# Weights' sums of the last three down passes made in DRAM by adding DMAs, ahead of time

## The chip, the cores and the metric

One Trainium2 chip, one of its cores. The metric is the device time of one execution in microseconds (us); the median of several runs counts.

## The reference, cut to what matters

One layer of a diffusion backbone over 1024 tokens of 1024 channels: a token mixer (Fourier groups and gated DeltaNet heads), then a ConvGLU channel mixer. The change lies in the channel mixer:

```python
p = h @ w_up_l                      # 1024 x 1024 by 1024 x 5632
val, gate = p[..., :D_FF], p[..., D_FF:]          # D_FF = 2816
gate = lax.conv_general_dilated(gate.reshape(bsz, rows, GRID_W, D_FF), w_dwc_l[:, :, None, :], ...)
return (jax.nn.silu(gate) * val) @ w_down_l       # 2816 x 1024
```

All arrays are float32, and so is the result.

## The kernel before, in words

Every matrix product is made of three: both operands are split into a high part (rounded to the type float32r) and the low rest, and `mm3` (L189) issues high x high (L191), high x low (L192) and low x high (L193). The high part is a cast on ACT, the low part a subtraction (`sub_l`, L164, its line in the profile is L165), on DVE or on POOL (GpSimd).

**Up products** (`ffn`, L1426, the loop at L1695). The hidden channels are 22 tiles of 128 (NF). For a channel tile f, seven products p = 1 to 7 over quarters of the operands replace eight (a Strassen-like scheme): `load(f)` (L1623) reads two pieces of w_up of 512 KB each on SP's queue, into the two buffers `raw` (even f) or into pages (odd f); `prepw(f, p)` (L1635) makes the sum of weights that p needs, on DVE or POOL, casts it on ACT into a buffer `wh` (four buffers) and subtracts on POOL into `wl`. It runs three products ahead (WA). A product is 12 matmuls. The tile x[5] of a channel tile gets x[7] added on POOL after p == 7 (L1729). DVE also makes the 3x3 convolution (L1472) and the gating, and 17 of the 22 gated tiles `g` are stored to DRAM (`gd`, L1482).

**Down products** (L1562 to L1617 and the loop at L1787). The product of the gated tiles with w_down is cut in the same way into 7 passes of 11 channels (NJ). A pass uses sums of two parts of the gate and sums of two blocks of w_down; `PASSES` lists them, as (half, part, sign) each:

```python
(((0, 0, 1), (1, 1, 1)), ((0, 0, 1), (1, 1, 1))), \
(((0, 1, 1), (1, 1, -1)), ((1, 0, 1), (1, 1, 1))), \
(((1, 0, 1), (0, 0, -1)), ((0, 0, 1), (0, 1, 1)))
```

These are the last three (numbers 4, 5 and 6 in the code): all three need a sum of two blocks of w_down. `prep(n)` (L1586) prepares channel j of a pass: it loads the blocks of w_down, 128 x 512, 256 KB each, on SP's queue (L1599), adds them on DVE (L1601), casts (L1608) and subtracts on DVE (L1609); then the same for the gate's parts: a sum on DVE (L1613), a cast (L1616), a subtraction on DVE (L1617). It is written five channels ahead of the products `mm(n, t)` (L1778), which make 12 matmuls per channel into four banks, t = 0 to 3. After a pass the banks are added up on DVE; the last sums of each output tile, its norm and the residual are in `early` (L1750) and `out` (L1756), which sit in a list `late` and are issued between channels. For the last six channels of the last pass the products are written bank by bank: all six for t = 0, then an addition of that bank (L1810) and `out(1, t)`, then t = 1 and so on.

Loads, gate parts, splits and results share a ring of 36 pages of 512 KB (`pg`, L143); `wh` and `wl` have four buffers each.

The order of the instructions on each engine is not fixed by the text alone. When the program is built, an ordering pass places instructions by when their operands and buffers are expected to be ready, and among those by the order of the text. `tc.issue_after(x)` holds the instructions of a block behind x on x's engine.

Of the kernel before, what the change touches and what calls it, by code (L numbers as in the profile page):

```python
# [9 lines left out]
F32 = mybir.dt.float32  # L10
# [3 lines left out]
ALU = mybir.AluOpType  # L14
# [4 lines left out]
P = 128  # L19
# [81 lines left out]
class Kern:  # L101
# [1324 lines left out]
    def ffn(self):  # L1426
        nc, tc, A = self.nc, self.tc, self.A
        V = nc.vector
        wu = A["w_up"][0].rearrange("(k p) n -> p k n", p=P)
        with tc.tile_pool(name="ffn", bufs=1, reuse_waits="tile") as fp:  # L1430
# [17 lines left out]
            def tt(eng, o, a, b, op=ALU.add):  # L1448
                eng.tensor_tensor(o, a, b, op=op)  # L1449
# [6 lines left out]
            def work(n):  # L1456
                for _ in range(n):
                    if back:
                        back.popleft()()
# [102 lines left out]
            PASSES = (((0, 0, 1), (0, 1, 1)), ((1, 1, 1),)), \  # L1562
# [6 lines left out]
            NJ = NF // 2  # L1569
# [4 lines left out]
            def gpart(f, i):  # L1574

                if f not in here:
                    here[f] = [f >= NF - 5] * 2
                    if not here[f][0]:
                        g[f] = self.pg()
                c = slice(512 * i, 512 * i + 512)  # L1580
                if not here[f][i]:
                    nc.sync.dma_start(g[f][:, c], gd[f][:, c])
                    here[f][i] = True
                return g[f][:, c]

            def prep(n):  # L1586

                ps, j = divmod(n, NJ)
                ga, wa = PASSES[ps]
                if ps == 4 and j == 0:  # L1590
                    self.gp2 = self.pg()
                    nc.sync.dma_start(self.gp2, self.gp[1])
                if n % 4:
                    raw = self.pg().rearrange("p (a n) -> p a n", a=2)
                else:
                    raw = self.wp.tile([P, 2, 512], F32, tag="raw", bufs=2, name=self.nm("wr"))
                for x, (k, c, _) in enumerate(wa):
                    f = j + NJ * k
                    nc.sync.dma_start(raw[:, x], A["w_down"][0, f * P:(f + 1) * P, 512 * c:512 * c + 512])  # L1599
                if len(wa) > 1:  # L1600
                    V.tensor_tensor(raw[:, 0], raw[:, 0], raw[:, 1], op=ALU.add if wa[1][2] > 0 else ALU.subtract)  # L1601
                if ps == 6 and j >= NJ - 6:
                    hl = self.page2()
                    wh, wl = hl[:, 0], hl[:, 1]
                else:
                    wh = self.wp.tile([P, 512], F32R, tag="wh", bufs=4, name=self.nm("wh"))
                    wl = self.wp.tile([P, 512], F32R, tag="wl", bufs=4, name=self.nm("wl"))
                nc.scalar.copy(wh, raw[:, 0])  # L1608
                self.sub_l(V, wl, raw[:, 0], wh)  # L1609
                src = [gpart(j + NJ * k, i) for i, k, _ in ga]  # L1610
                if len(ga) > 1:
                    tmp = big("s") if ps == 0 else tmps[n % 4]
                    V.tensor_tensor(tmp, src[0], src[1], op=ALU.add if ga[1][2] > 0 else ALU.subtract)  # L1613
                    src = [tmp]
                gs = self.page2()
                nc.scalar.copy(gs[:, 0], src[0])  # L1616
                self.sub_l(V, gs[:, 1], src[0], gs[:, 0])  # L1617
                return gs, wh, wl
# [4 lines left out]
            def load(f):  # L1623
                if f >= NF or f in raws:
                    return
                raws[f] = []
                for col in (DFF + f * P, f * P):
                    if f % 2:
                        r = self.pg().rearrange("p (k n) -> p k n", k=ND)
                    else:  # L1630
                        r = self.wp.tile([P, ND, P], F32, tag="raw", bufs=2, name=self.nm("wr"))
                    nc.sync.dma_start(r, wu[:, :, col:col + P])
                    raws[f] += [flat(r[:, 0:4]), flat(r[:, 4:8])]

            def prepw(f, p, paged=False):  # L1635
                a00, a01, a10, a11 = raws[f]
                S = Ss.setdefault(f, {})
                e = (V, nc.gpsimd)
                if p in (1, 2, 4):
                    src = {1: a00, 2: a01, 4: a11}[p]  # L1640
                else:
                    src = S[p] = big("s")
                    a, b = {5: (a10, a11), 6: (S.get(5), a00), 3: (a01, S.get(6)), 7: (a00, a10)}[p]
                    tt(e[(8 if f > 9 else 160) >> p & 1], src, a, b, ALU.add if p == 5 else ALU.subtract)
                if paged:
                    hl = self.page2()
                    h, l = hl[:, 0], hl[:, 1]
                else:
                    h = self.wp.tile([P, 512], F32R, tag="wh", bufs=4, name=self.nm("wh"))
                    l = self.wp.tile([P, 512], F32R, tag="wl", bufs=4, name=self.nm("wl"))  # L1650
                nc.scalar.copy(h, src)  # L1651
                self.sub_l(nc.gpsimd, l, src, h)
                W[f, p] = h, l

            load(2)
            for f in range(2):
                pvs[f][1], pvs[f][3] = self.psum(tags[f][1]), self.psum(tags[f][3])
# [37 lines left out]
            for n, (f, p) in enumerate(seq):  # L1695
                if n + WA < len(seq):
                    f2, p2 = seq[n + WA]
                    load(f2)
                    if p2 == 1:
                        load(f2 + 1)  # L1700
                    prepw(f2, p2)
                x = st.setdefault(f, {})
                bank = {2: "B", 5: "C", 3: "C"}.get(p, "A")
                if p in (1, 2, 5):
                    x[bank] = self.psum({"A": "g", "B": "mm", "C": "mm"}[bank])
                ps = x[bank]
                h, l = W.pop((f, p))
                for d in range(4):
                    c = slice(d * P, d * P + P)
                    b = B[p][d]  # L1710
                    self.mm3(ps, h[:, c], l[:, c], b[:, 0], b[:, 1], start=(d == 0 and p in (1, 2, 5)), stop=(d == 3),
                             skip_group_check=True)
                if p in (1, 5, 6, 7):
                    x[p] = big("m")
                    nc.scalar.copy(x[p], ps)
                pad = pads[f % 2]
                if p == (6 if f == 2 else 2):

                    while f - 2 not in convd:
                        work(1)  # L1720
                    r = lambda t: t.rearrange("p (r c) -> p r c", c=64)
                    tt(V, pad[:, 5:13, 1:65], r(x["B"]), r(x[1]))
                if p == 3:
                    for o, c in ((1, 0), (13, 256)):
                        r = lambda t: t[:, c:c + 256].rearrange("p (r c) -> p r c", c=64)
                        tt(V, pad[:, o:o + 4, 1:65], r(ps), r(x[6]))
                    finish(f, lambda i, x=x: (x["A"], x[5])[i])
                if p == 7:
                    tt(nc.gpsimd, x[5], x[5], x[7])  # L1729
                work(2 + (len(back) > 14))  # L1730
                if n >= len(seq) - 7:
                    for _ in range(3):
                        if order:
                            gpart(order.pop(0), 0)
                if n >= len(seq) - 4:
                    i = len(ops)
                    ops[i] = prep(i)
            work(len(back))
            for i in range(5):
                if i not in ops:  # L1740
                    ops[i] = prep(i)
# [45 lines left out]
            for ps in range(7):  # L1787
                bk = banks[BSET[ps]]
                for j in range(NJ):
                    n = ps * NJ + j  # L1790
                    a = 5
                    if ps == 6 and j >= 5:
                        a += j - 5 + 1
                    for i in range(n + 5, min(n + a, NS - 1) + 1):
                        if i not in ops:
                            ops[i] = prep(i)
                    if n < NS - 6:
                        for t in range(4):
                            mm(n, t)
                    if late and j > 0 and (ps < 6 or len(late) > 4 or j % 5 == 5 - 1):  # L1800
                        late.pop(0)()
                    if ps in (5, 6) and j >= NJ - 5 and len(ahead) < 4 * (ps - 4):
                        load_x1(len(ahead))
# [9 lines left out]
                if ps in (0, 2, 3):  # L1813
                    name = {0: "M5", 2: "C01", 3: "C10"}[ps]
# [58 lines left out]
```

## Time and profile before

| | |
|---|---|
| median of 3 runs | 1364.43 us (1362.92 to 1364.84) |
| the profiled execution | 1366.19 us |
| its span, first to last instruction | 1364.4 us |
| mean granted TensorE clock | 0.983 of full speed |
| PE (matmul) busy | 1285.0 us, 94% |
| DVE (VectorE) busy | 992.6 us, 73% |
| ACT (ScalarE) busy | 641.1 us, 47% |
| POOL (GpSimd) busy | 472.2 us, 35% |
| POOL's own DMA queue | 864 packets, 3.15 MB |

The profile is of one execution, taken by the hardware profiler; its times count from the first instruction. PE is the matmuls, PEld the weight loads that run beside them, SP the engine whose queue issues nearly all DMAs. Up products run from about 765 to 1121 us, the down passes from about 1130 to 1346 us, 30 us each. A matmul's end is modelled, so a busy PE says that products are in flight, not that the engine is at its peak; the distance of their starts says more.

### The profile page before, as it was taken

To read this page: it belongs to the slowest core of one execution; us is meant where nothing else is said; L and a number is where in the kernel's file an instruction comes from. 1 tells how busy PE (TensorE), PEld (TensorE's weight loads), DVE (VectorE), ACT (ScalarE), POOL (GpSimd) and SP (SyncE) were. 2 spreads that over 40 slices of the span, in tenths; PEclk is the share of its full clock that TensorE was granted. 3 is DMA by queue.
4 is the path that set the end of the run, shared out by engine and by line. 5 is a ranking of instruction groups with operands and counts; after the bars stand their busy time and mean duration, and the time that the engine had idled before them with its cause. 6 is when DMAs were issued, how large, how long until landed. Compare 5 with 4: busy or idle time off the path is not lost.

```text
span 1364.4 us, 19307 instructions
## 1 busy us (share of the span) xinstructions
PE 1285.0 (94%) x6678; PEld 1025.0 (75%) x6678; DVE 992.6 (73%) x1802; ACT 641.1 (47%) x1334; POOL 472.2 (35%) x464
## 2 busy tenths in 40 slices
PE   5999999989899999898999899999999999999994
PEld 2677886667557789786777688888888887888873
DVE  2465555944963856857469899888888889878997
ACT  5553456532554233444757444444444445555342
POOL 0221114332434252542126667665666650000000
PEclk9999999999999999999999899999999999999997
DMA  9622226676476778825432233332233166645665
GB/s 333 179 107 71 74 77 193 209 220 209 150 201 236 273 229 275 269 64 172 163 131 79 77 94 93 93 93 66 59 92 93 47 208 231 201 137 165 201 216 185
DMA packets 183732, 213.67 MB, mean 157 GB/s; under 512 B 31640, under 2 KB 119762, under 8 KB 183634
## 3 DMA queue, kind: packets, MB, share of 16 engines
q1 hardware_dynamic: 182769, 209.28, 47.8%
q0 software_dynamic: 864, 3.15, 0.7%
q8 instruction: 53, 0.87, 0.3%
q14 instruction: 46, 0.37, 0.1%
HBM read 163.11 MB, written 49.28 MB: 156 GB/s over the span
## 4 chain that ended last, share of the span: by engine, by line
PE 56%; DVE 22%; DMA 8%; issue 5%; ACT 5%; POOL 2%; SPq 1%; DVEq 0%; POOLq 0%; ACTq 0%
PE ps L191 14%; PE ps L193 14%; PE ps L192 14%; DVE cv L1472 4%; PE ps L1082 3%; DVE T L983 2%; DVE pg L985 2%; PE ps L305 2%; PE ps L1026 2%; DVE pg L1449 1%; DVE wl L165 1%; DVE pg L165 1%; PE ps L1013 1%; DVE s L1449 1%; DMA pg<-in_x_dram 1%
## 5 line engine op out<-in xcount | busy, mean ns | idle before, releaser
L191 PE MATMUL ps<-pg,wh 128*128 128x512 f32 (+1 forms) x896 | 351.7, 393 | 7.6 <-DVE pad L1449 5.2
L192 PE MATMUL ps<-pg,wh 128*128 128x512 f32 (+1 forms) x896 | 346.2, 386 | 0.0
L193 PE MATMUL ps<-pg,wl 128*128 128x512 f32 (+1 forms) x896 | 346.2, 387 | 0.0
L1472 DVE SCALAR_TENSOR_TENSOR cv<-pad,dw,cv 128x1024 f32<-128x1024 f32 x176 | 226.3, 1286 | 11.6 <-ACT cv L1470 8.2
L191 PEld LDWEIGHTS ps<-pg,wh 128*128 128x128 f32 x896 | 169.8, 190 | 56.1 <-issue 20.7
L193 PEld LDWEIGHTS ps<-pg,wl 128*128 128x128 f32 x896 | 169.7, 189 | 35.7 <-issue 3.5
L192 PEld LDWEIGHTS ps<-pg,wh 128*128 128x128 f32 x896 | 170.2, 190 | 30.9 <-issue 0.4
L165 POOL TENSOR_TENSOR wl<-wr,wh 128x512 fp32r<-128x512 f32 x68 | 89.4, 1322 | 188.7 <-ACT wh L183 158.0
L165 POOL TENSOR_TENSOR wl<-s,wh 128x512 fp32r<-128x512 f32 x80 | 107.7, 1349 | 62.2 <-ACT wh L1651 61.9
L1651 ACT CAST wh<-s 128x512 fp32r<-128x512 f32 x80 | 49.6, 621 | 120.1 <-PE ps L192 116.0
L191 PE MATMUL ps<-pg,pg 128*128 128x512 f32 (+1 forms) x248 | 98.5, 399 | 3.3 <-ACT pg L1616 1.8
L191 PE MATMUL ps<-wh,pg 128*128 128x512 f32 x250 | 97.8, 393 | 2.0 <-ACT pg L1616 1.7
L192 PE MATMUL ps<-pg,pg 128*128 128x512 f32 (+1 forms) x248 | 97.5, 395 | 1.0 <-POOL pg L165 0.7
L193 PE MATMUL ps<-pg,pg 128*128 128x512 f32 (+1 forms) x248 | 96.8, 395 | 1.4 <-DVE pg L355 0.8
L192 PE MATMUL ps<-wl,pg 128*128 128x512 f32 x250 | 97.6, 390 | 0.0
L193 PE MATMUL ps<-wh,pg 128*128 128x512 f32 x250 | 97.3, 390 | 0.0
L1082 PE MATMUL ps<-pg,pg 128*128 128x128 f32 x464 | 58.4, 277 | 0.7 <-ACT pg L1142 0.6
L191 PEld LDWEIGHTS ps<-pg,pg 128*128 128x128 f32 x248 | 47.7, 192 | 14.9 <-ACT pg L1616 2.2
L193 PEld LDWEIGHTS ps<-pg,pg 128*128 128x128 f32 x248 | 47.5, 193 | 13.8 <-issue 1.7
L1082 PEld LDWEIGHTS ps<-pg,pg 128*128 128x128 f32 x464 | 54.9, 192 | 2.7 <-ACT pg L1142 1.0
L192 PEld LDWEIGHTS ps<-pg,pg 128*128 128x128 f32 x248 | 47.8, 193 | 11.2 <-POOL pg L165 1.1
L191 PEld LDWEIGHTS ps<-wh,pg 128*128 128x128 f32 x250 | 46.9, 188 | 12.3 <-ACT pg L1616 2.1
(363 smaller groups left out, 2434.5 us busy)
## 6 DMA issues: line engine op xcount, KB each, us to landing
pg<-in_w_down_dram SPq DMA_DIRECT2D x97, 256.0 KB, 4.5
wr<-in_w_ada_dram SPq DMA_DIRECT2D x32, 512.0 KB, 4.5
wr<-in_w_up_dram SPq DMA_DIRECT2D x24, 512.0 KB, 3.8
wr<-in_w_in_dram SPq DMA_DIRECT2D x20, 512.0 KB, 4.3
pg<-in_w_up_dram SPq DMA_DIRECT2D x20, 512.0 KB, 5.4
wr<-in_w_down_dram SPq DMA_DIRECT2D x35, 256.0 KB, 2.7
gd<-pg SPq DMA_DIRECT2D x17, 512.0 KB, 2.7
pg<-gd SPq DMA_DIRECT2D x34, 256.0 KB, 4.6
```

The source lines that it names most:

```text
L165: eng.tensor_tensor(l, full, h.bitcast(F32), op=ALU.subtract)
L191: nc.tensor.matmul(out, ah, bh, start=start, stop=False, **kw)
L192: nc.tensor.matmul(out, ah, bl, start=False, stop=False, **kw)
L193: nc.tensor.matmul(out, al, bh, start=False, stop=stop, **kw)
L305: nc.tensor.matmul(ps[32 * j:32 * j + 32, :], self.csil[:, k, :], t[:, a, :], start=(k < 4), stop=(k >= 4), skip_group_check=True, tile_po ...
L983: V.tensor_tensor(tmp, L[:nl, j + 1:, j:j + 1].broadcast_to([nl, r, c]), X[:nl, j:j + 1, 0:c].broadcast_to([nl, r, c]), op=ALU.mult)
L985: V.tensor_tensor(X[:nl, j + 1:, 0:c], X[:nl, j + 1:, 0:c], tmp, op=ALU.subtract)
L1026: nc.tensor.matmul(ps[po, h * n:(h + 1) * n], Q[k0:k0 + kn, d, h, po], R[k0:k0 + kn, d, h, c0:c0 + n], start=True, stop=True, skip_group_c ...
L1082: nc.tensor.matmul(ps[:, hs(h)], lhs(h), rhs(h), start=True, stop=True, skip_group_check=True)
L1449: eng.tensor_tensor(o, a, b, op=op)
L1472: V.scalar_tensor_tensor(c3, src, w, c3, op0=ALU.mult, op1=ALU.add)
L1651: nc.scalar.copy(h, src)
```

## The change

While the up products run, the sums of two blocks of w_down that the last three passes need, 33 tiles of 128 x 512, are made in DRAM: after p == 7 of a channel tile, two blocks are copied from w_down to DRAM tiles `wsum` by SP (behind the last load of w_up that has been written), and at the p == 7 of the next channel tile the second blocks are added to them by two DMAs that POOL issues, right behind its addition of x[7]. `prep` of the last three passes then loads one tile and leaves out its own addition. The addition on POOL is the same as before; only its handle is passed on.

```diff
+            wsum, todo = {}, [(ps, j) for ps in (4, 5, 6) for j in range(NJ)]
+            half = []
+
+            def wblock(ps, j, x):
+                k, c, s = PASSES[ps][1][x]
+                assert s > 0
+                f = j + NJ * k
+                return A["w_down"][0, f * P:(f + 1) * P, 512 * c:512 * c + 512]
+
+            def wsums(pool):
+
+                with tc.issue_after(pool.ins):
+                    for q in half:
+                        nc.gpsimd.dma_start(wsum[q], wblock(*q, 1), accum_op=ALU.add)
+                half.clear()
+                with tc.issue_after(self.loaded.ins):
+                    while todo and len(half) < 2:
+                        q = todo.pop(0)
+                        wsum[q] = self.drp.tile([P, 512], F32, name=self.nm("wsum"))
+                        nc.sync.dma_start(wsum[q], wblock(*q, 0))
+                        half.append(q)
...
+                if (ps, j) in wsum:
+                    nc.sync.dma_start(raw[:, 0], wsum[ps, j])
+                    wa = ()
                 for x, (k, c, _) in enumerate(wa):
...
-                    nc.sync.dma_start(r, wu[:, :, col:col + P])
+                    self.loaded = nc.sync.dma_start(r, wu[:, :, col:col + P])
...
                 if p == 7:
-                    tt(nc.gpsimd, x[5], x[5], x[7])
+                    wsums(nc.gpsimd.tensor_tensor(x[5], x[5], x[7], op=ALU.add))
```

## Rows read from the trace of the kernel before

**Rows 1.** Busy time by stretch: PE, PEld, DVE, ACT, POOL; clock, DMA share, GB/s.

```profile
1222.00:1252.00 30.00, 30.00 (x134) 24.86 (x133) 22.95 (x37) 16.92 (x34) 0.00 (x0) 1.00 0.55 178
1252.00:1282.00 30.00, 30.00 (x134) 24.83 (x133) 29.08 (x49) 14.75 (x30) 0.00 (x0) 1.00 0.51 165
1282.00:1311.60 29.60, 29.60 (x132) 24.54 (x131) 29.60 (x51) 11.96 (x21) 0.00 (x0) 1.00 0.79 265
...
1325.20:1346.00 20.80, 18.78 (x73) 14.29 (x72) 15.77 (x43) 7.14 (x17) 0.00 (x0) 0.92 0.30 103
1346.00:1364.40 18.40, 0.05 (x1) 0.00 (x0) 14.56 (x48) 2.56 (x11) 0.00 (x0) 0.61 0.63 228
```

**Rows 2.** The same stretches for L1601 alone: DVE busy (executions), clock, DMA.

```profile
1252.00:1282.00 30.00, 7.39 (x11) 1.00 0.51 165
1282.00:1311.60 29.60, 5.44 (x8) 1.00 0.79 265
1311.60:1325.20 13.60, 2.70 (x4) 1.00 0.57 196
1325.20:1346.00 20.80, 2.65 (x4) 0.92 0.30 103
```

**Rows 3.** Timeline of PE, 1326 to 1346 us: start, length, instruction.

```profile
1326.38 0.39 PE L193 MATMUL ps<-pg,pg 128*128 128x512 f32 x1
1328.52 0.50 PE L191 MATMUL ps<-pg,pg 128*128 128x512 f32 x1 [1.75 <-ACT pg L1616]
...
1332.96 0.40 PE L191 MATMUL ps<-pg,pg 128*128 128x512 f32 x1
...
1339.54 0.84 PE L191 MATMUL ps<-pg,pg 128*128 128x512 f32 x3
...
1345.66 0.39 PE L193 MATMUL ps<-pg,pg 128*128 128x512 f32 x1
```

**Rows 4.** Timeline of DVE, 1290 to 1361 us.

```profile
1290.37 0.68 DVE L1601 TENSOR_TENSOR pg<-pg 128x512 f32<-128x512 f32 x1
1290.97 0.68 DVE L165 TENSOR_TENSOR wl<-wr,wh 128x512 fp32r<-128x512 f32 x1
...
1343.14 1.29 DVE L1449 TENSOR_TENSOR pg<-ps,pg 128x512 f32<-128x512 f32 x2 [4.26 <-PE ps L193]
...
1358.54 0.16 DVE L203 RECIPROCAL sums<-rsq 128x1 f32<-128x1 f32 x1
...
1359.32 0.75 DVE L1769 SCALAR_TENSOR_TENSOR pg<-m,sums,pg 128x512 f32<-128x512 f32 x1
1359.98 0.75 DVE L1769 SCALAR_TENSOR_TENSOR pg<-pg,sums,pg 128x512 f32<-128x512 f32 x1
```

**Rows 5.** The page's costliest groups, up products: busy, mean ns, idle before, releaser.

```profile
L165 POOL TENSOR_TENSOR wl<-s,wh 128x512 fp32r<-128x512 f32 x80 | 107.7, 1349 | 62.2 <-ACT wh L1651 61.9
L1651 ACT CAST wh<-s 128x512 fp32r<-128x512 f32 x80 | 49.6, 621 | 120.1 <-PE ps L192 116.0
```

**Rows 6.** Timeline of SP's queue there: loads of w_up for the next tile.

```profile
989.88 1.48 SPq L1632 DMA_DIRECT2D pg<-in_w_up_dram  x2
```

**Rows 7.** Timeline of POOL in the up products: two successive additions of x[7].

```profile
994.80 1.74 POOL L1449 TENSOR_TENSOR m<-m,m 128x512 f32<-128x512 f32 x1
...
1013.84 1.30 POOL L1449 TENSOR_TENSOR m<-m,m 128x512 f32<-128x512 f32 x1
```

**Rows 8.** DMAs that POOL issues (L531): ns min/median/max on POOL, first and last start.

```profile
L531 POOL DMA_DIRECT2D pg<-in_ftab_dram x6: 528/542/720, 65.6 to 120.2; - x6
```

**Rows 9.** The page's DMA issues: count, KB each, median us to landing.

```profile
pg<-in_w_up_dram SPq DMA_DIRECT2D x20, 512.0 KB, 5.4
...
gd<-pg SPq DMA_DIRECT2D x17, 512.0 KB, 2.7
```

**Rows 10.** Busy time in the up products, columns as in rows 1.

```profile
765.00:850.00 85.00, 85.00 (x374) 70.25 (x373) 75.92 (x76) 37.79 (x59) 56.50 (x43) 0.99 0.33 95
850.00:1121.00 271.00, 270.52 (x1192) 223.33 (x1191) 224.57 (x231) 118.73 (x184) 169.92 (x129) 1.00 0.29 89
```

## The prediction

> **What bounds the kernel now.** I read the stage table first. In the down products PE is busy through whole stretches (30.00 of 30 us in the fourth and fifth pass); only the last 39 us show PE missing: 18.78 us busy of 20.8, then 18.4 us in which it runs nothing [rows 1]. So up to 1325 us the end is set by TensorE, and an engine that gets less to do there gives nothing by itself. But in the same table DVE goes from 22.95 of 30 us (1222 to 1252) to 29.08 of 30 and then 29.60 of 29.6: from the fifth pass on it falls behind. The second table says what the removed line costs there: 11, 8, 4 and 4 adds in the four stretches from 1252 on; the other 6 of the 33 lie just before [rows 2].
>
> Next the timeline of PE. The last six channels make 72 products, 0.227 us apart where nothing is late. Six are issued, then PE stands 1.75 us for the split of a gate sum (ACT L1616, fed by DVE), and after that it issues at 0.43 us and comes back to 0.23 only at 1332.96 (the granted clock of that stretch is 0.92 [rows 1]). From 1326.38 to 1332.96 there are ten steps in 6.58 us in place of 2.27: **4.3 us lost**. The row at 1339.54 shows three L191 in a row, where the text of the kernel writes L191, L192, L193 for one bank: the products were issued in the order in which their operands came, channel by channel, so that no bank closed before the end [rows 3].
>
> Last the timeline of DVE. Back to back its 512-column operations start 0.60 us apart (1290.37, 1290.97). In the tail it stands 4.26 us until 1343.14 for the first bank of the last pass, adds two banks together there, and works nearly without a pause to 1360.73, 14.7 us after the last product's end (1345.66 + 0.39) [rows 3, 4]. The span ends 3.7 us later. So **the end is DVE's tail**, started late.
>
> **The change part by part.**
>
> *Adds off DVE.* 33 operations of 0.60 us go, 19.8 us of DVE. Until 1325 PE covers them: worth nothing there. In passes 4 to 6 a channel then takes three such operations (1.8 us) and not four (2.4), against 12 products of 0.227 = 2.72 us on PE. The pass before, which already has one load, no weights' sum and three operations per channel, runs PE at 30.00 of 30 with DVE at 22.95 [rows 1]: that is my model for the new passes. With the late work on top, 1252 to 1311.6 would hold 58.7 - 19 x 0.60 = 47.3 us of DVE in 59.6. DVE then keeps its lead, the stall goes, and with it the low clock: PE ends 4.3 us earlier, its last product at 1341.7.
>
> *The tail.* Two bounds. From PE: after the last bank one add (0.68), the square on ACT (by the cast of as many columns, 0.62 [rows 5], and 0.2 for reading its sum), eight small steps of 0.2 (1358.54 to 1359.32 has four), two multiply-adds, 0.66 and 0.75, and the 3.7 us of store and end [rows 4]: about 8.3 us with PE's 0.39, so 1350.0. From DVE: its end, 1360.73, less the 4.26 us of standing (banks that close one by one, four us apart, give it work), less the 8 adds after 1311.6 (4.8), less what it was behind at 1311.6. This last is between nothing and three channels, the most that four `wh` buffers let it run ahead: 3 x 1.8 = 5.4; I take the middle, 2.7. That gives 1349.0, and 1352.7 with the end. The small steps of four tiles can no longer all hide behind other tiles' work: 0 to 4 x 0.78 = 3.1, I take 1.5. **Span 1354.2**, between 1350.0 and 1355.4 + 3.1 = 1358.5.
>
> *Loads in the passes.* One load per channel in place of two, of the same 256 KB, from a tile that was written some 100 us before: the same queue does less, no cost.
>
> *Copies on SP.* 33 issues, at most two per channel tile, by 0.5 us each at most (two larger ones took 1.48 [rows 6]) on a queue that mostly waits in the up products. They stand behind the loads just issued and ahead of the next ones; the channel tile takes 19.04 us (994.80 to 1013.84), so 1 us or so costs nothing [rows 7].
>
> *Adding DMAs on POOL.* Nothing in the trace adds in a DMA. The nearest row is POOL's own loads, which hold it 0.53 to 0.72 us each [rows 8]; I take 0.54, the median: two are 1.1 us per channel tile. From the other side, POOL could be held until the transfer has landed: a load and a store of 512 KB, 5.4 + 2.7 = 8.1 us [rows 9]. Cover: POOL is busy 169.92 of 271 us, and 56.50 of 85 [rows 10], which leaves 7.1 and 6.4 us per tile. What is queued behind the adds is the next low part of the weights (`wl`, 1.35 us). Where POOL waits, it is for ACT's cast, and that for PE to give a buffer back [rows 5]; with four buffers the split is due 3 x 2.72 = 8.2 us after the release, of which cast and subtraction take 2.0 (0.62 + 1.35). So POOL may be held **6.2 us** at one place before PE stands; 1.1 us is hidden. Nobody waits for the adds' landing: by the code the last one goes out two channel tiles before the up products end, and the first sum is loaded in the fourth pass after them, some 100 us later.
>
> A rule of the Trainium skill speaks against this part. In "SBUF — State Buffer", section "SBUF: two separate sides", a DMA that POOL issues can't get its descriptors written while VectorE runs an operation that holds the shared ports, and the next section gives about 3100 ns in place of 620. By it two adds would hold POOL 6.2 us, all that there is, so that every microsecond of waiting for a copy would come on top: the sum would stay, but the slower rival below would have a third of the chances. The page's section "Who interferes with whom" says that a tensor-tensor operation has no such mode, and no DMA that POOL issues in this trace holds it more than 0.72 us [rows 8].
>
> *Traffic.* DMA's share is 0.29 to 0.33 in the up products [rows 10]. Copies and adds move 1 to 1.5 MB per tile beside the 1.5 MB of loads and gate stores there, so it rises to some 0.5 to 0.65; hidden.
>
> **The sum.** The profiled execution took 1366.19 us for a span of 1364.4, 1.8 around it, and lies 1.76 above the median of the runs. So a span of 1354.2 is about 1354.2 us of median: 10.2 us less.
>
> **Rivals.**
>
> *Only the stall goes* (the products stay in the order by channel and the banks close together): DVE stays the tail, the gain is the 4.3 us: 1360.1. For it: the order is fixed when the program is built, by what the ordering thinks is late, which no row shows. Against: that order answers to the late operands of the last channels, and these come from DVE. Chance 0.20.
>
> *Loads take DVE's place.* A weight's page is given back by the DVE subtraction of an earlier channel, and the load behind it takes some microseconds; if this ring is the limit, the last channels come as late as before. Then DVE only waits where it added: gain 0 to 2.7, about 1363. Against it is the pass before, which runs through with the same single load [rows 1]. Chance 0.14.
>
> *POOL stands for the copies: slower.* POOL works in order, and an add waits until its copy has landed. For even channel tiles the second load of the weights goes out late: in the shown tile the next tile's loads follow it at 989.88, and POOL comes to the adds after the sum of 994.80, at 996.5 [rows 6, 7]. A copy that lands in 2.7 us is there; one that goes behind the two loads (issued to 991.4, 5.4 us) and takes 8.1 itself lands at 1004.9 and holds POOL 8.4 us, with 1.1 for the issues 9.5. Over 6.2 us PE stands: 3.3 us in each of nine even tiles, 30 us, less the 10 won: 1384. It decides from a landing after about 1001.6. For: the issue is only 5 to 7 us ahead. Against: the copy is half as big as the loads that give 8.1, and was written first. Chance 0.14, dearer adds on POOL included (they decide from 3.1 us each).
>
> **How the numbers follow.** Forecast 0.52 (1350 to 1358.5), stall only 0.20, loads 0.14, POOL 0.14. A measurement of this kernel tells about 0.2%, 2.7 us, from no change. Faster by more: forecast and stall only, 0.72. Within: the loads' case, 0.14. Slower: 0.14. The range goes from 1348.5, a little under PE's bound, to 1366, which takes in both smaller cases and leaves out the slower one and some of the edges: 8 in 10. The likeliest case alone is 1350 to 1358.5.
>
> **What would show it.** Right: 22 of the 55 executions of L1601 left, DVE near 27 of 30 us in passes 4 to 6, no wait of PE near 1326 and full clock to its last product near 1342, the last pass's adds on DVE about four us apart and not two together, some 10 us between the last product and the span's end, and PE at 50 of 50 us in the up products with POOL holding each add under 1 us. Wrong: PE idle in the up products behind `wl`, POOL's DMA rows above 3 us or a wait of POOL for the copies above 5; or a tail that still takes 18 us after PE's end, with the last pass's adds together.

## The result, and the profile after

The kernel after takes 1382.07 us (median of four runs, 1379.31 to 1387.89), the one before 1364.29 us in the same session: a ratio of 1.0136, 95% interval 1.0112 to 1.0160. It is **slower by 17.8 us**; the forecast was 10.2 us faster, and the result lies outside the range. The profiled execution, the slowest of the four, took 1387.89 us for a span of 1386.1.

Where the time went shows when the program is cut at two places that both kernels have: the product with which the loop over channel tiles starts (PE waits 5.2 us for DVE's `pad` there), and the first product of the down passes. First the kernel before, then the kernel after; the columns are those of [rows 1].

```profile
761.43:1126.67 365.24, 364.76 (x1597) 301.11 (x1597) 308.98 (x318) 161.93 (x252) 228.99 (x173) 0.99 0.31 94
```

```profile
768.22:1162.51 394.29, 374.97 (x1597) 305.12 (x1597) 328.91 (x318) 159.50 (x252) 257.72 (x206) 0.97 0.49 130
1162.51:1376.71 214.20, 212.47 (x937) 175.23 (x935) 183.99 (x320) 106.06 (x202) 1.66 (x1) 1.00 0.49 165
...
1330.00:1376.71 46.71, 46.71 (x208) 38.68 (x206) 38.48 (x93) 19.53 (x43) 0.00 (x0) 1.00 0.44 155
1376.71:1386.10 9.39, 0.39 (x2) 0.00 (x0) 5.54 (x18) 1.13 (x4) 0.00 (x0) 0.66 0.42 154
```

The down passes did what was hoped. From their first product to the end they take 223.6 us (1386.1 - 1162.51) in place of 237.7 (1364.4 - 1126.67): 14.1 us less. PE runs 46.71 of the last 46.71 us, where it had the hole and the lower clock of [rows 1, 3], and behind its last product there are 9.4 us in place of 18.7 (1364.4 - 1345.66). **The up products lost 29.1 us**, 394.29 in place of 365.24. Of these PE stands 18.8 more (394.29 - 374.97 = 19.32 against 0.48) and is busy 10.2 longer with the same 1597 products, at a granted clock of 0.97. DVE is busy 328.91 us in place of 308.98 with the same 318 operations. The other 6.8 us lie ahead of the loop, where only the first two copies are new; the start of the loop lies between 757.1 us (small adds) and 768.2 in the fourteen profiles taken here, with copies and adds at 759.3 and 767.0 in two profiles of one kernel (e8, e11), so I read these 6.8 us as spread from run to run. The order of the instructions is not the cause: in the two traces the operations of the up products stand in the same order on DVE (318), ACT (252) and POOL (173), and so do the products on PE.

DVE's timeline in the tail of the kernel after, beside [rows 4]:

```profile
1364.90 0.69 DVE L1449 TENSOR_TENSOR pg<-ps,pg 128x512 f32<-128x512 f32 x1 [3.79 <-PE ps L193]
...
1369.99 0.68 DVE L1449 TENSOR_TENSOR pg<-ps,pg 128x512 f32<-128x512 f32 x1
...
1373.34 0.67 DVE L1449 TENSOR_TENSOR pg<-ps,pg 128x512 f32<-128x512 f32 x1
...
1377.83 0.68 DVE L1449 TENSOR_TENSOR pg<-ps,pg 128x512 f32<-128x512 f32 x1
```

The last pass's banks now close one by one, 3.4 to 5.1 us apart, and not two together at the start of the tail.

What PE waited for in the up products (waits: engine, line, releaser; us in total, times, longest) was ACT's copy of a bank into `m` (L1741, before L1715), not the low parts that the prediction watched. Before:

```profile
PE ps L191 <- ACT m L1715: 0.5, 2, 0.3
...
ACT pg L1476 <- DVE cv L1472: 25.1, 20, 3.1
...
DVE s L1449 <- POOL wl L165: 13.4, 15, 3.6
```

After:

```profile
PE ps L191 <- ACT m L1741: 19.3, 14, 3.9
...
ACT pg L1476 <- DVE cv L1472: 74.1, 21, 6.8
...
DVE s L1449 <- POOL wl L165: 23.7, 17, 3.2
```

(Both from 765 us to the first product of the down passes.) Read from the bottom, this is a chain: DVE's sums `s` wait for POOL's low parts, the convolution taps behind them on DVE come late, ACT stands in front of the SiLU (L1476) for the last tap, and the copy that gives PE its bank back is queued behind that SiLU. One turn of it, in the timeline of the kernel after (the worst of the loop; start, length, instruction, what it waited for):

```profile
978.21 1.64 POOL L1600 DMA_DIRECT2D wsum<-in_w_down_dram  x2
...
978.94 4.01 DVE L1449 TENSOR_TENSOR s<-wr 128x512 f32<-128x512 f32 x1 [2.52 <-DMA wr<-in_w_up_dram]
979.30 3.09 POOL L165 TENSOR_TENSOR wl<-s,wh 128x512 fp32r<-128x512 f32 x2
...
993.07 1.02 ACT L1476 ACTIVATE pg<-cv 128x1024 f32<-128x1024 f32 x1 [6.83 <-DVE cv L1472]
...
994.50 0.59 ACT L1741 COPY m<-ps 128x512 f32<-128x512 f32 x1
...
995.14 0.79 PE L191 MATMUL ps<-pg,wh 128*128 128x512 f32 x1 [3.94 <-ACT m L1741]
995.73 0.63 PE L192 MATMUL ps<-pg,wh 128*128 128x512 f32 x1
```

and the same place in the timeline of the kernel before, around the first row of [rows 7]:

```profile
993.58 1.81 DVE L1449 TENSOR_TENSOR s<-wr 128x512 f32<-128x512 f32 x1
...
996.50 1.30 POOL L165 TENSOR_TENSOR wl<-s,wh 128x512 fp32r<-128x512 f32 x1
...
998.99 1.31 POOL L165 TENSOR_TENSOR wl<-s,wh 128x512 fp32r<-128x512 f32 x1 [1.18 <-ACT wh L1651]
...
1005.53 1.03 ACT L1476 ACTIVATE pg<-cv 128x1024 f32<-128x1024 f32 x1 [1.19 <-DVE cv L1472]
```

Before, POOL goes from the addition of x[7] straight to a `wl` and has **1.18 us** to spare only before the next one. The pair of adds takes 1.64. The two `wl` behind it then run without a break until 982.39 (979.30 + 3.09; the first one's record begins while the second add still runs). DVE's sum lies beside them, ends 0.56 us after them, and takes 4.01 us where it took 1.81. Add the 2.52 us by which its load was late, and SiLU waits 6.83 us in place of 1.19. PE then stands 3.94 us, and its next products are 0.43 us apart and not 0.23, at a granted clock of 0.52 of full speed, about the lower of the two levels (1.2 of 2.4 GHz):

```profile
995.14:1001.00 5.86, 5.86 (x14) 4.62 (x15) 5.27 (x6) 2.30 (x4) 2.53 (x3) 0.52 0.57 175
```

The adding DMAs (ns min/median/max on POOL; us to landing), a group of the page and its DMA issues answer to [rows 8, 5, 9]:

```profile
L1600 POOL DMA_DIRECT2D wsum<-in_w_down_dram x33: 785/852/1115, 793.1 to 1127.9; - x33
...
DMA to landing us min/median/max: 4.0/5.7/9.6
```

```profile
L165 POOL TENSOR_TENSOR wl<-s,wh 128x512 fp32r<-128x512 f32 x80 | 119.8, 1565 | 29.5 <-ACT wh L1677 24.4
```

```profile
pg<-in_w_up_dram SPq DMA_DIRECT2D x20, 512.0 KB, 7.4
```

Two adds together hold POOL 1.64 us, 0.82 each, not 0.54 (the record of the second begins in the first, so the median of single records, 0.85, is a little high); no wait of POOL for a copy is in the trace. POOL's idle time in front of this group of `wl` halved, from 62.2 to 29.5 us. Their mean grew from 1349 to 1565 ns, in part because the records of those behind an add begin before it ends. Loads of w_up into pages land after 7.4 us in place of 5.4 [rows 9].

### The profile page after: what moved, and what is told of

It is laid out like the page before. It is cut to its first block, busy times and chain, and to the rows that moved or that the text cites. A ratio compares the mean times of both kernels' runs of the same rounds, so it can differ in the third digit from the quotient of the medians.

```text
span 1386.1 us, 19334 instructions
## 1 busy us (share of the span) xinstructions
PE 1294.8 (93%) x6673; PEld 1029.9 (74%) x6678; DVE 996.4 (72%) x1769; ACT 638.2 (46%) x1334; POOL 501.7 (36%) x497
## 3 DMA queue, kind: packets, MB, share of 16 engines
HBM read 171.76 MB, written 66.58 MB: 172 GB/s over the span
## 4 chain that ended last, share of the span: by engine, by line
PE 37%; DVE 21%; issue 6%; DMA 5%; ACT 5%; POOL 4%; SPq 0%; DVEq 0%; ACTq 0%; POOLq 0%
PE ps L191 9%; PE ps L192 9%; PE ps L193 9%; DVE cv L1472 7%; DVE s L1449 3%; PE ps L1082 2%; DMA wr<-in_w_up_dram 2%; PE ps L1026 2%; DVE pg L1449 1%; POOL wl L165 1%; DVE T L983 1%; PE cv L191 1%; PE cv L193 1%; PE cv L192 1%; DVE pg L985 1%
## 5 line engine op out<-in xcount | busy, mean ns | idle before, releaser
L191 PE MATMUL ps<-pg,wh 128*128 128x512 f32 (+1 forms) x896 | 355.1, 397 | 26.3 <-ACT m L1741 20.7
L165 POOL TENSOR_TENSOR wl<-s,wh 128x512 fp32r<-128x512 f32 x80 | 119.8, 1565 | 29.5 <-ACT wh L1677 24.4
L1082 PEld LDWEIGHTS ps<-pg,pg 128*128 128x128 f32 x464 | 56.9, 198 | 4.5 <-DVE pg L1144 2.4
L1476 ACT ACTIVATE pg<-cv 128x1024 f32<-128x1024 f32 x22 | 22.6, 1028 | 81.7 <-DVE cv L1472 81.7
L193 PEld LDWEIGHTS ps<-pg,pg 128*128 128x128 f32 x248 | 47.4, 192 | 13.6 <-DVE pg L355 1.9
L165 POOL TENSOR_TENSOR wl<-pg,wh 128x512 fp32r<-128x512 f32 x30 | 39.2, 1305 | 50.4 <-ACT wh L1677 50.4
L191 PEld LDWEIGHTS ps<-pg,pg 128*128 128x128 f32 x248 | 47.5, 191 | 12.6 <-ACT pg L351 1.3
```

The costliest lines, as they stand in the source:

```text
L165: eng.tensor_tensor(l, full, h.bitcast(F32), op=ALU.subtract)
L191: nc.tensor.matmul(out, ah, bh, start=start, stop=False, **kw)
L193: nc.tensor.matmul(out, al, bh, start=False, stop=stop, **kw)
L1082: nc.tensor.matmul(ps[:, hs(h)], lhs(h), rhs(h), start=True, stop=True, skip_group_check=True)
L1476: nc.scalar.activation(g[f], self.cv, AF.Silu)
```

## The experiments

Theory P: POOL's time. What costs is that POOL is held behind the addition of x[7]. Theory T: traffic. What costs are the bytes of copies and adds (DMA share 0.49 in place of 0.31), which make the loads late. Theory D: the DMAs themselves cost on POOL's queue, beyond the time they hold it. All ratios are to the kernel before on the same chip, with the 95% interval; up and down are the two parts cut as above, from the profiled execution of each. That execution need not be a middling one: it is the slowest of four for the kernel after, the slowest of ten for e11, and the fastest of nine for e3 and for e10.

| kernel | median us (runs) | ratio | up us | down us |
|---|---|---|---|---|
| before | 1364.29 (4) | | 365.2 | 237.7 |
| after | 1382.07 (4) | 1.0136 [1.0112, 1.0160] | 394.3 | 223.6 |
| e1, one block | 1355.73 (6) | 0.9927 [0.9902, 0.9952] | 366.5 | 223.7 |
| e2, copies on SP alone | 1351.97 (3) | 0.9901 [0.9870, 0.9932] | 365.4 | 224.3 |
| e3, small adds | 1381.68 (9) | 1.0123 [1.0102, 1.0143] | 386.1 | 223.8 |
| e4, all in the down passes | 1371.93 (10) | 1.0043 [1.0020, 1.0066] | 365.0 | 242.3 |
| e5, adds in gaps | 1364.79 (10) | 0.9999 [0.9979, 1.0020] | 376.3 | 223.9 |
| e6, adds in the down passes | 1372.11 (5) | 1.0043 [1.0025, 1.0061] | 367.5 | 246.6 |
| e7, sum on POOL | 1375.83 (4) | 1.0093 [1.0059, 1.0127] | 365.4 | 246.3 |
| e8, one add per tile | 1356.42 (2) | 0.9938 [0.9914, 0.9961] | 369.5 | 223.8 |
| e9, one add, in a gap | 1359.99 (12) | 0.9958 [0.9939, 0.9978] | 372.2 | 223.8 |
| e10, POOL held, no DMA | 1372.45 (9) | 1.0042 [1.0022, 1.0063] | 383.6 | 223.4 |
| e11, e8 again | 1359.14 (10) | 0.9956 [0.9942, 0.9969] | 369.8 | 223.7 |
| e12, last pass alone | 1360.78 (12) | 0.9963 [0.9947, 0.9980] | 371.6 | 226.5 |

Diffs are to the kernel after, unless they say otherwise.

**One block.** No sums, copies or adds.

```diff
-                if (ps, j) in wsum:
-                    nc.sync.dma_start(raw[:, 0], wsum[ps, j])
-                    wa = ()
+                if ps > 3:
+                    wa = wa[:1]
...
-                    wsums(nc.gpsimd.tensor_tensor(x[5], x[5], x[7], op=ALU.add))
+                    nc.gpsimd.tensor_tensor(x[5], x[5], x[7], op=ALU.add)
```

> Leaves out the second block of w_down in the last three passes: no copies, no adding DMAs, no sum, one load per channel. Both theories (POOL's time; traffic) say that the up products then take what they took before, 365 us from the wait before the loop to the first down product (changed kernel: 394), and that the down part keeps the changed kernel's 224 us (before: 238): 1350 us in all. If the up products stay long, neither theory holds, and the cause is the order of instructions.

Up 366.5 and down 223.7: with the sum gone and nothing put in its place, the down part is that of the kernel after, and the up part that of before. So the gain of the down part comes from DVE's 33 sums, and the loss of the up part from copies or adds.

**Copies on SP alone.** Both blocks are moved by plain DMAs that SP issues: as many bytes read and written as in the kernel after (171.76 and 66.58 MB of DRAM in both), nothing on POOL; the sum is left out.

```diff
-                with tc.issue_after(pool.ins):
-                    for q in half:
-                        nc.gpsimd.dma_start(wsum[q], wblock(*q, 1), accum_op=ALU.add)
...
+                        other = self.drp.tile([P, 512], F32, name=self.nm("wsec"))
+                        nc.sync.dma_start(other, wblock(*q, 1))
```

> Leaves out the sum: SP copies both blocks to DRAM, POOL issues nothing; the passes load the first copy. POOL's time theory (the adds hold POOL 1.6 us per tile, which delays the sums of weights on DVE, the SiLU on ACT and the banks of PE): up products at 365 us, 1350 us in all. Traffic theory (copies and adds make the loads of w_up land late): up products at 380 us or more, 1365 or more.

**Small adds.** Copies and adds of 8 of the 512 columns: the same instructions, 1/64 of the bytes; the second block is left out of the passes.

```diff
-                        nc.gpsimd.dma_start(wsum[q], wblock(*q, 1), accum_op=ALU.add)
+                        nc.gpsimd.dma_start(wsum[q][:, :8], wblock(*q, 1)[:, :8], accum_op=ALU.add)
...
-                        nc.sync.dma_start(wsum[q], wblock(*q, 0))
+                        nc.sync.dma_start(wsum[q][:, :8], wblock(*q, 0)[:, :8])
...
-                if (ps, j) in wsum:
...
+                if ps > 3:
+                    wa = wa[:1]
```

> Copies and adds are as many, in the same places, but of 8 columns in 512: hardly any traffic, nearly the same descriptors; the passes load the first block alone (the second is left out). POOL's time theory: up products still 385 to 394 us, 1370 to 1380 in all. Traffic theory: 365 us and 1350.

The pair settles the traffic. The up products (columns as in [rows 1]) with the bytes and without the adds, then with the adds and hardly a byte:

```profile
760.10:1125.46 365.36, 364.75 (x1597) 301.17 (x1598) 306.09 (x318) 161.86 (x252) 229.09 (x173) 0.99 0.45 139
```

```profile
757.14:1143.19 386.05, 373.17 (x1596) 303.25 (x1597) 327.24 (x318) 159.05 (x252) 257.28 (x206) 0.98 0.32 90
```

and that kernel's adds on POOL (ns min/median/max):

```profile
L1600 POOL DMA_DIRECT2D wsum<-in_w_down_dram x33: 781/840/1105, 782.4 to 1108.6; - x33
```

A DMA share of 0.45 costs PE 0.6 us of 365; a share of 0.32 with the adds costs it 12.9 us of standing, and 386.1 us in all. That is 21 of the 29 us lost, in the fastest of nine executions; by the medians the small adds cost what the large ones do (1.0123 and 1.0136, and the intervals overlap). Theory T falls: bytes cost nothing in the up products that these runs show. A small add holds POOL as long as a large one, 0.84 against 0.85 us.

**POOL held, without a DMA.** From the one-block kernel; in the 17 channel tiles in which the kernel after issues adds, POOL fills the page it has just read with zeros.

```diff
                    nc.gpsimd.tensor_tensor(x[5], x[5], x[7], op=ALU.add)
+                    if 2 < f < 20:
+                        for _ in range(3):
+                            nc.gpsimd.memset(x[7], 0.0)
```

> No sums, no copies, no adding DMAs; the second block of weights is left out in the last three passes. In 17 channel tiles POOL instead fills the page of m's that it has just read with zeros, three times 128x512, about 1.5 us together, where the pair of adding DMAs stood (they held it 1.6 us). If it is the time for which POOL is held there, the up products go from 366.5 us (one block, nothing on POOL) to 380 to 394, PE waits for ACT's copy of m 10 to 20 us, and the time is 1370 to 1382. If it is something that only a DMA on POOL's queue does (its descriptors, its traffic), the up products take 365 to 368 us and the time is about 1355.

Busy times of its up products, its waits there, and the memsets (ns min/median/max):

```profile
758.91:1142.47 383.56, 370.33 (x1597) 300.76 (x1597) 326.88 (x318) 158.42 (x252) 257.56 (x224) 0.99 0.30 90
```

```profile
PE ps L191 <- ACT m L1740: 13.2, 17, 2.2
...
ACT pg L1476 <- DVE cv L1472: 69.4, 20, 5.8
```

```profile
L1757 POOL MEMSET m<- x51: 524/526/530, 783.7 to 1108.6; 128x512 f32 x51
```

1.58 us of plain work on POOL (3 x 0.526) acts as the pair of adds does: DVE is busy 326.88 us, SiLU waits 69.4 us against 74.1, PE stands 13.2 us behind the same copy of `m`, and the up products take 383.6 us, 17.1 more than with one block and nothing on POOL. **Theory P stands**, without a DMA; theory D alone would have left the up products at 365 to 368. But it does not carry the whole loss. By the medians and ratios of all runs, each against the kernel before on its own chip, the memsets cost 16 to 18 us over one block, the small adds 26 to 27, and the intervals of the two lie apart (1.0042 [1.0022, 1.0063] and 1.0123 [1.0102, 1.0143]). The other 8 to 11 us come with the adds themselves and not with their bytes; what they may be stands under "Not settled".

**Dose and place.** Three kernels vary how much POOL is held at once. In the first all 33 adds stay, but singly, behind two subtractions at which POOL had idle time; in the second there is one add per tile behind the addition of x[7], 19 sums, and the other 14 stay on DVE; the third has one per tile, 18 sums, behind one of those subtractions.

```diff
-                with tc.issue_after(pool.ins):
-                    for q in half:
-                        nc.gpsimd.dma_start(wsum[q], wblock(*q, 1), accum_op=ALU.add)
+                ready.extend(half)
...
-                self.sub_l(nc.gpsimd, l, src, h)
+                sub = nc.gpsimd.tensor_tensor(l, src, h.bitcast(F32), op=ALU.subtract)
+                if p in (1, 4) and ready:
+                    with tc.issue_after(sub.ins):
+                        q = ready.pop(0)
+                        nc.gpsimd.dma_start(wsum[q], wblock(*q, 1), accum_op=ALU.add)
```

> All 33 copies and adds stay in the up products, two per channel tile, but each add stands alone behind the low part of p = 1 or p = 4, where POOL waited 1.4 us for ACT in the kernel before. If it is where POOL is held that counts (its time of 0.8 us falls into a wait), up products come back to 365 to 370 us and the whole to 1350 to 1356. If two adds per tile cost the same wherever they stand (POOL's sum of time, or the adds' traffic), they stay at 385 to 394 and 1372 to 1380.

```diff
-            wsum, todo = {}, [(ps, j) for ps in (4, 5, 6) for j in range(NJ)]
+            wsum, todo = {}, [(5, j) for j in range(3, NJ)] + [(6, j) for j in range(NJ)]
...
-                    while todo and len(half) < 2:
+                    while todo and len(half) < 1:
```

> One copy and one add per channel tile in place of two, behind the same addition of x[7]; 19 sums (the last pass and eight of the pass before), the other 14 on DVE. POOL's time theory, if the cost goes with POOL's time: half the loss in the up products, 378 to 380 us. If there is slack for one add and not for two: 365 to 370. The down part should be a little longer than 224, 226 to 230.

The third is the second with j from 4 on, and with the add moved as in the first, behind p == 1 alone:

```diff
+                if p == 1 and ready:
+                    with tc.issue_after(sub.ins):
+                        nc.gpsimd.dma_start(wsum[ready[0]], wblock(*ready.pop(0), 1), accum_op=ALU.add)
```

> One sum per channel tile, 18 in all (the whole last pass and seven of the pass before; the other 15 stay on DVE), and the adding DMA stands behind the subtraction that makes the low part of the first product's weights, a tile after its copy, where POOL waits for ACT. If POOL's time just behind the sum of the m's is what costs, the up products fall from the 369.5 us of the run with one add there to 365.5 to 367, ACT waits for DVE's cv before SiLU about 35 us in place of 44.6, and the time is 1351 to 1354. If any add on POOL costs the same wherever it stands, up products 369 to 370 and 1356 to 1358.

> The version with one copy and one add per channel tile behind the sum of the m's (19 sums) once more, on the same chip as the version with the add in the gap. 1355 to 1358, up products 368 to 371 us; about 3 us over the version with the add in the gap if the place matters with one add too, the same time within 0.2% if it does not.

Waits of the second kernel (e8) in its up products, and its busy times there:

```profile
PE ps L191 <- ACT m L1741: 2.3, 3, 1.8
...
ACT pg L1476 <- DVE cv L1472: 37.0, 20, 5.4
```

```profile
759.31:1128.81 369.50, 367.22 (x1596) 302.35 (x1597) 308.91 (x318) 161.52 (x252) 247.25 (x191) 0.99 0.44 117
```

(The 44.6 us in the expectation above count one wait more, 7.6 us, that lies behind the up products.) Two adds at once cost 29 us, the same two apart 11, one alone 4 to 7. The dose is not linear: about 0.8 us fits into the 1.18 us that POOL has behind that addition, 1.6 does not. With one add there DVE is busy 308.91 us, as before the change, and from 883 to 1054 us a channel tile takes the 19.04 us of before. The loss sits in one place, at 841 to 847 us, where PE stands 1.78 us and goes on at the lower clock. With one add the place made no difference that the medians show: 1359.99 and 1359.14 us, up 372.2 and 369.8; my 365.5 to 367 for the gap was a miss. In the trace of the gap PE stands 0.61 us in every second tile. So the rule "put it where POOL waits" holds for the pair but is not a gain in itself. Two more forecasts were off: the pair in gaps took neither 365 to 370 us nor 385 to 394, and with 19 sums the down part kept 223.8 us where I had 226 to 230.

**Other places for the sums.** Copy and add one per channel in the first down passes; copies in the up products and adds in the down passes; no DMA, but the former addition made by POOL (diff to the kernel before).

```diff
+                    with tc.issue_after(self.loaded.ins):
...
+                    nc.gpsimd.dma_start(wsum[q], wblock(*q, 1), accum_op=ALU.add)
...
+                    if n > 3:
+                        wsums()
```

> The same sums by the same copies and adds, but one per channel in the first down passes, where POOL has nothing to do. Both theories: up products at 365 us. POOL's time theory: the whole down gain stays, 1350 to 1353 us. Traffic theory: the first passes, which load two blocks per channel at a DMA share of 0.6, get late: 1355 to 1370.

```diff
+                if n > 4 and ps < 4 and ready:
+                    with tc.issue_after(nc.gpsimd.tensor_copy(tiny[:, :1], raw[:, 0, :1]).ins):
+                        q = ready.pop(0)
+                        nc.gpsimd.dma_start(wsum[q], wblock(*q, 1), accum_op=ALU.add)
```

> The copies stay in the up products, two per tile, and the 33 adds go to the first down passes, one per channel, each behind a one-column copy on POOL that waits for that channel's load. By POOL's time the up products are at 365 us. The down part tells what the adds' own traffic is worth there: 224 to 226 us (1350 to 1353 in all) if the copies were half of what filled the queues in the run that did both there, 235 or more (1362) if the adds alone fill them.

```diff
-                    V.tensor_tensor(raw[:, 0], raw[:, 0], raw[:, 1], op=ALU.add if wa[1][2] > 0 else ALU.subtract)
+                    (nc.gpsimd if ps > 3 else V).tensor_tensor(raw[:, 0], raw[:, 0], raw[:, 1], op=ALU.add if wa[1][2] > 0 else ALU.subtract)
```

> The kernel before with one edit: the sums of the last three passes are made by POOL in SBUF, no DRAM tiles and no adding DMAs. Up products as before, 365 us. If DVE's time alone makes the late end, the down part is at 224 to 226 us (1350 to 1353). If two-input operations of DVE and POOL hold each other up, as the sums in the up products seem to, DVE's operations get longer and the part stays at 230 to 238 (1356 to 1364).

All three leave the up products alone (365.0 to 367.5) and lose in the down passes. Copies and adds there (242.3 us, 1371.93 in all) and the sum on POOL (246.3) ended above the dearer of the two forecasts made for each, 1370 and 238. The kernel with the copies ahead and only the adds there, in the early passes: busy times, and a wait of DVE.

```profile
1170.00:1200.00 30.00, 23.18 (x92) 17.15 (x91) 16.11 (x27) 7.55 (x15) 8.52 (x15) 0.94 0.96 243
1200.00:1230.00 30.00, 22.90 (x88) 17.98 (x87) 16.91 (x29) 8.47 (x17) 9.68 (x16) 0.87 0.86 191
```

```profile
DVE wr L1626 <- DMA wr<-in_w_down_dram: 20.1, 4, 6.4
```

The DMA engines are busy 0.96 and 0.86 there (0.57 and 0.40 in the run with copies on SP alone), DVE waits for its weights, and PE runs 23 of 30 us. Here traffic does cost, as far as these waits tell. Then the sum on POOL: groups of the two engines that share the work, in the down passes.

```profile
L165 DVE TENSOR_TENSOR pg<-pad,pg 128x512 fp32r<-128x512 f32 x44 | 41.1, 942 | 2.9 <-ACT pg L1616 2.8
...
L1601 POOL TENSOR_TENSOR pg<-pg 128x512 f32<-128x512 f32 x24 | 46.9, 1972 | 15.9 <-DMA pg<-in_w_down_dram 11.7 <-DVE s L1449 2.4 <-DVE wl L165 1.8
```

POOL's sum takes 1.97 us, and DVE's subtractions beside it 942 ns where they take 686 in the run with copies on SP alone. What DVE is relieved of it pays back.

**The last pass alone.** From the version with one add per tile: 11 sums.

```diff
-            wsum, todo = {}, [(5, j) for j in range(3, NJ)] + [(6, j) for j in range(NJ)]
+            wsum, todo = {}, [(6, j) for j in range(NJ)]
```

> Copies and adding DMAs for the last pass's 11 sums alone, one per channel tile in the first 11 tiles, behind the sum of the m's; the 22 sums of the two passes before stay on DVE. If the gain of the down part comes from the last pass, where PE has 12 products of 0.227 us per channel and DVE falls behind, it keeps its 223.7 to 225 us and the up products take 367 to 368: 1352 to 1356, a little under the version with 19 sums. If DVE has to gain its lead already in the pass before, the down part takes 228 to 235 us, the tail behind PE's last product is 12 us or more, and the time is 1358 to 1364.

Down 226.5 us: a third of the sums brings 11.2 of the 14.1 us, with 10.2 us behind the last product. That lies between my two forecasts, 223.7 to 225 and 228 to 235. The up part did not fall under that of 19 sums (371.6 against 369.8), so nothing is won on the whole; the two intervals lie over each other. The gain sits in the last pass, but not all of it.

## Why the prediction was wrong

**Adds off DVE, and the stall: right.** PE needs 214.2 us from its first to its last product of the down part in place of 219.0 (1345.66 - 1126.67): 4.8 won, 4.3 forecast. L1627, the former L1601, runs 22 times, all before 1238, and DVE has 54.21 of 60 us from 1270 on: 27 of 30, as written. One reading was wrong, on the safe side: the stretch taken as the model, 1222 to 1252 us, held six of the old sums itself, 4.13 of DVE's 22.95 us.

**The tail: right in kind, mis-sized.** I took the bound from DVE, 12.5 us behind the last product, and PE's bound, 8.3, for the lower end (its parts add up to about 8.5); it is 9.4. So the down part won 14.1 and not 10.2. What I had put on top for work left over at 1311.6 and for small steps that nothing hides did not show.

**Loads in the passes, copies on SP: right.** The two plain copies per sum cost nothing in the up products.

**Adding DMAs on POOL: the step that failed.** The instruction's price was off by 0.3 us (0.82 for 0.54). That counts against the 1.18 us that POOL has at this place: two at 0.54 might just have fitted, which was not tested. But the prediction would have let 6.2 us pass there, and so the larger mistake was the cover. That POOL may be held 6.2 us at one place before PE stands, and that 1.1 us is hidden, followed one path only, from POOL's low part to PE's next product. That path is not in the list of PE's waits after the change. The other customer of POOL's low parts is DVE: its sums `s` need the buffers that `wl` reads, already waited for them 13.4 us before the change, and pass any delay to the taps, to SiLU and, since ACT works in order, to the copy that frees PE's bank. On that path the nearest idle time of POOL is 1.18 us, and the 7 us per tile that I counted lie elsewhere in the tile.

The rule of the Trainium skill that I weighed was the wrong one of its page. In "SBUF — State Buffer", section "Who interferes with whom", I had read that tensor-tensor operations have no such mode and stopped there. The same section says that a VectorE operation with two inputs in SBUF does contend with a GpSimd operation that reads SBUF, and not with one that only writes. The traces agree. One group of DVE's sums beside POOL's subtractions, before and after (780 to 1110 us), grew from 790 to 1491 ns:

```profile
L1449 DVE TENSOR_TENSOR s<-s,pg 128x512 f32<-128x512 f32 x9 | 7.1, 790 | 0.2 <-POOL wl L165 0.2
```

```profile
L1449 DVE TENSOR_TENSOR s<-s,pg 128x512 f32<-128x512 f32 x8 | 11.9, 1491 | 12.0 <-POOL wl L165 12.0
```

And in the run with memsets a sum that began beside them took its usual 0.69 us, the next, beside two `wl`, 1.38:

```profile
968.12 1.70 POOL L1757 MEMSET m<- 128x512 f32 x3
968.39 0.69 DVE L1449 TENSOR_TENSOR s<-wr 128x512 f32<-128x512 f32 x1 [2.16 <-DMA wr<-in_w_up_dram]
...
969.78 2.56 POOL L165 TENSOR_TENSOR wl<-s,wh 128x512 fp32r<-128x512 f32 x2
971.51 1.38 DVE L1449 TENSOR_TENSOR s<-s,wr 128x512 f32<-128x512 f32 x1
```

So the adds cost DVE twice: it waits for POOL, and POOL's `wl`, pushed together, stretch its sums (the 19.9 us more of busy time, 328.91 for 308.98). The other rule, with its figure of about 3100 ns for a DMA that POOL issues, shows nowhere: 33 adds took 0.785 to 1.115 us.

**Traffic: right in the up products as far as tested** (0.45 of share for nothing), and no licence for the down passes.

**The rival with POOL** gave the right sign and nearly the sum (30 us lost, less 10: 1384), but by luck, for its mechanism did not occur: POOL never waited for a copy. Its side remark, dearer adds that decide from 3.1 us each, was too high by more than three times: 0.82 each decides, if two stand together.

**Not settled.** Why a delay of about half a microsecond per tile grows to 1.7 us per tile (29 / 17) was read, not tested. In the trace the load of the next tile's weights stands on SP's queue behind the gate's store, which waits for SiLU, so a late SiLU makes the next sum late: 2.52 us in the turn shown, and 14.1 us over the up products of the kernel with memsets, which has no added traffic. Moving that load ahead of the store was not tried.

The 29 us are also not spread evenly. From one addition of x[7] to the next the kernel after takes 19.4 to 20.7 us from 897 to 1107 us (19.0 to 19.5 before), but 25.3 in two of these turns. One is shown above; here are an ordinary turn and the other long one:

```profile
938.42 1.65 POOL L1600 DMA_DIRECT2D wsum<-in_w_down_dram  x2
938.54 0.69 DVE L1449 TENSOR_TENSOR s<-wr 128x512 f32<-128x512 f32 x1 [1.89 <-POOL m L1755]
...
1063.13 1.63 POOL L1600 DMA_DIRECT2D wsum<-in_w_down_dram  x2
1063.50 4.36 DVE L1449 TENSOR_TENSOR s<-wr 128x512 f32<-128x512 f32 x1 [2.16 <-DMA wr<-in_w_up_dram]
1064.22 3.08 POOL L165 TENSOR_TENSOR wl<-s,wh 128x512 fp32r<-128x512 f32 x2
```

Where DVE's sum began 0.12 us after the first add it took 0.69 us; where it began 0.37 or 0.73 after, it was done only after both `wl`. The small adds have one such turn, the memsets none, and there a sum that began 0.91 us after the first memset still took 0.69. So a few of these turns, about 6 us each, may be what the adds cost beyond the memsets. Why a sum is caught in this way was not tested: beside a single add, with no `wl` right behind it, sums took 0.68 to 0.69 us too (the kernels with adds in gaps).

The lower clock makes some 6 of the 29.1 us: 39 steps between products are 0.36 to 0.50 us long, 7.7 us over the usual 0.227, where the kernel before has 10, 2.0 us over it.

**The better version.** One add per tile, 19 sums, beats both kernels: 0.9938 [0.9914, 0.9961] and, in a second session, 0.9956 [0.9942, 0.9969]; about 6 us under the kernel before. With nothing on POOL, and the sum left out, 13.5 us is what there would be to win.

## What to carry to other kernels

Cover for work put on a half idle engine is the idle time **behind the instruction where it is put**, on the path of every customer of that engine, not its idle share and not the path to TensorE alone; look for a customer that already waits for it a little. An engine that works in order hands a small delay to unrelated work queued behind it, here the copy that frees a bank. Look also at what the work behind it is pushed against: here two subtractions on POOL stretched DVE's sums. And try half the dose: 0.8 us per tile cost 4 to 7 us in all, 1.6 us cost 29 (17 as plain work).

## What the runs showed of the hardware

- An adding DMA from DRAM to DRAM takes POOL 0.84 us for 4 KB and 0.85 for 256 KB (medians of the records; two in a row 1.64); a plain load took it 0.54.
- With one copy and one add per channel in the down passes the DMA share went to 1.08, the 16 engines' packets lying over each other, while only 319 GB/s were moved; [rows 1] has 265 GB/s at 0.79.
- POOL's 128x512 addition took 1.97 us beside a busy DVE, and DVE's own subtractions there 942 ns and not 686. A two-input sum of DVE beside POOL's subtractions took up to 4.36 us, beside memsets 0.69.
